# A two-layer encoder with retrieved experts: 32 dense tokens' w_up products turned into row gathers, and sparse gathers brought forward into the retrieval

## The chip, the cores and the metric

The kernel runs on one core of a Trainium2 chip. The metric is the device time of one execution in microseconds (us), the median of the runs shown. A profile is one execution taken by the hardware profiler; its engines are PE (TensorE matmuls; PEld are its weight loads), DVE (VectorE), ACT (ScalarE), POOL (GpSimd) and SP (SyncE, which here only issues DMAs). Each engine works through its own queue in order.

## The reference, cut to what matters

512 tokens of width 1024 pass through two layers. Layer 0 mixes tokens by neighbourhood attention, layer 1 by a short convolution; after either comes the same expert block ("peer"), which takes most of the time:

```
q = (xc @ w_query).reshape(c, PEER_HEADS, 2, PEER_HALF_DIM)
sc = jnp.einsum('chpd,hpnd->chpn', q, keys32)
sv, si = lax.top_k(sc, PEER_TOPK)
...
best, pos = lax.top_k(cand, PEER_TOPK)
eidx = jnp.take_along_axis(cidx, pos, axis=-1)
g = jax.nn.softmax(best, axis=-1)
u = w_up[eidx]
a = jnp.einsum('cd,chkd->chk', xc, u)
act = jax.nn.gelu(a, approximate=False) * g
vv = w_down[eidx]
return jnp.einsum('chk,chkd->cd', act, vv)
```

Every token picks 8 x 16 = 128 of 16384 experts; an expert is one row of w_up and one of w_down (1024 floats each).

## The kernel before, in words

The 512 tokens are four chunks of 128. Chunk 3 is the **sparse** chunk: for each of its 128 picks k, POOL gathers one row per token from w_up (an indirect DMA of 512 KB into `row`), DVE multiplies it with the normed tokens `hn` and sums (`sq`, L482), and later a gather from w_down is added to `accg` (L491). Those are 256 gathers in each layer. Chunks 0 to 2 (TD = 384 tokens) are **dense**: all 16384 experts are computed for all 384 tokens, and a gate matrix that is zero where an expert wasn't picked masks the rest.

The dense part of a layer runs over 128 blocks of 128 experts. An **up** (`dense_up`) loads 512 KB of w_up, splits it into a rounded half on ACT (`wu_h`) and the rest on DVE (`wu_l`, L106), and runs 24 matmuls with 384 columns (`ps_up`, L127), whose Gelu goes to `ab`; the first NPRE = 52 blocks are parked in DRAM (`ad`). A **down** (`dense_down`) multiplies `ab` with the gates `gt`, splits the product and 512 KB of w_down (`wd_l`), and runs 18 matmuls with 512 columns into six PSUM banks that stay open over the layer (`acc`, L541).

A layer of the expert block runs through these stages. In the **query** stage 16 blocks of w_query are multiplied and DVE takes top-16 lists. In the **selection**, DVE works for each chunk through `select`, some 80 small instructions, which give picks and gates. In the **gate products**, for each four dense tokens (a quad, 96 in all) DVE builds one-hot matrices from the picks (`ob`, `oa`), scaled by the gate on ACT or DVE, PE multiplies them (`ps_gb`, four float32 matmuls, two records each in the profile), and ACT copies the result to `stage`, from which `gd` is written to DRAM. In the **experts** stage the downs of all 128 blocks run, the ups that are left and the 256 gathers.

Ups of the first 52 blocks are interleaved with selection and gate products by a planner's ratio: `retrieval` yields estimates of DVE and PE time, and ups are put in until PE's estimate reaches PRE_RATE times that of DVE. In the experts stage ups run AHEAD blocks ahead, and gathers are spread by LATE. Tiles come from pools with a set number of buffers (`wu_h` 2, `wu_raw` and `wd_raw` 3), and a scheduler that estimates times itself places each engine's instructions in their final order, so the order below is that of the built program and not of the source.

## Time and profile before

| what | value |
|---|---|
| median of 3 runs | 2993.33 us (2993.03 to 2993.86) |
| profiled execution, own time | 2994.69 us |
| its span (first to last instruction) | 2992.9 us |
| PE busy | 2952.2 us (99%) |
| DVE busy | 2345.6 us (78%) |
| ACT busy | 1360.9 us (45%) |
| POOL busy | 663.4 us (22%) |

Own time is 1.8 us more than the span and 1.4 us above the median of the runs. Busy time of PE counts a matmul that waits in the pipeline as busy, so how dense PE is must be read from the distance between matmuls, not from its share.

### The profile page before, as it was taken

What the parts mean: (1) busy time and instruction counts of PE and PEld (TensorE: products, weight loads), DVE (VectorE), ACT (ScalarE), POOL (GpSimd) and SP (SyncE); (2) the same over time, 40 slices, a digit from 0 to 9 for tenths busy, and PEclk for the clock granted to TensorE, in tenths of its full rate; (3) what the DMA queues carried; (4) which work ended last, traced back from release to release, by engine and by line L of the source; (5) the groups of instructions that cost most, each with busy time, mean ns of one, the idle gap of its engine ahead of it and who ended that gap; (6) DMA issues with size and microseconds to landing.
All of it is one profiled execution on the core that took longest, in us unless ns stands there. A gap on an engine that the chain in (4) does not pass through costs nothing.

```text
span 2992.9 us, 43780 instructions
## 1 busy us (share of the span) xinstructions
PE 2952.2 (99%) x15570; PEld 2636.1 (88%) x15570; DVE 2345.6 (78%) x5115; ACT 1360.9 (45%) x2237; POOL 663.4 (22%) x571
## 2 busy tenths in 40 slices
PE   8999999999999999999999999999999999999998
PEld 6777899999888888888878789999988888888886
DVE  5445999886888888878864489998788888888786
ACT  5453257994333333333332323699733333333333
POOL 0000000002343444343400000000043434444341
PEclk9999999999999999999999999999999999999999
DMA  5323355659999999999933324556799999999995
GB/s 187 106 81 96 95 161 168 240 214 328 335 337 346 335 343 329 337 343 324 320 113 93 117 87 129 166 216 217 261 352 348 334 347 332 338 330 346 325 329 190
DMA packets 297979, 747.93 MB, mean 250 GB/s; under 512 B 23456, under 2 KB 139168, under 8 KB 294688
## 3 DMA queue, kind: packets, MB, share of 16 engines
q1 hardware_dynamic: 224032, 476.67, 46.5%
q0 software_dynamic: 73728, 268.47, 24.7%
q8 instruction: 122, 2.00, 0.3%
q14 instruction: 97, 0.79, 0.1%
HBM read 672.17 MB, written 72.88 MB: 249 GB/s over the span
## 4 chain that ended last, share of the span: by engine, by line
PE 91%; DVE 4%; issue 2%; DMA 2%; ACT 1%; POOL 0%; DVEq 0%; POOLq 0%; SPq 0%
PE ps_up L127 45%; PE acc L541 33%; PE ps_gb L462 6%; PE ps_o L191 3%; DVE wu_l L106 1%; PE ps_k L403 1%; PE ps_s L260 1%; PE ps_o L300 1%; DMA row<-in_up,eidx 1%; PE ps_pt L286 1%; DMA gd<-stage 0%; PE ps_t L175 0%; POOL row L475 0%; DVE tk L600 0%; ACT sq L150 0%
## 5 line engine op out<-in xcount | busy, mean ns | idle before, releaser
L127 PE MATMUL ps_up<-xhf,wu_l 128*128 128x384 f32 (+1 forms) x2304 | 798.4, 347 | 1.1 <-DVE wu_l L106 1.0
L127 PE MATMUL ps_up<-xhf,wu_h 128*128 128x384 f32 (+1 forms) x2304 | 794.3, 345 | 2.3 <-ACT ab L504 2.0
L127 PE MATMUL ps_up<-xlf,wu_h 128*128 128x384 f32 (+1 forms) x2304 | 792.4, 344 | 0.0
L105 ACT ACTIVATE wu_h<-wu_raw 128x1024 fp32r<-128x1024 f32 x336 | 355.4, 1058 | 688.8 <-PE ps_up L127 413.2
L475 POOL DMA_INDIRECT row<-in_up,eidx x256 | 325.1, 1270 | 1277.9 <-DMA wu_raw<-in_up_t 848.5
L541 PE MATMUL acc<-wd_h,w_l 128*128 128x512 f32 x1536 | 601.4, 392 | 0.1
L541 PE MATMUL acc<-wd_l,w_h 128*128 128x512 f32 x1536 | 601.2, 391 | 0.0
L105 ACT ACTIVATE wd_h<-wd_raw 128x1024 fp32r<-128x1024 f32 x256 | 271.5, 1061 | 699.2 <-issue 591.0
L106 DVE TENSOR_TENSOR wu_l<-wu_raw,wu_h 128x1024 fp32r<-128x1024 f32 x336 | 411.1, 1224 | 191.2 <-ACT wu_h L105 190.1
L541 PE MATMUL acc<-wd_h,w_h 128*128 128x512 f32 x1536 | 513.0, 391 | 0.9 <-ACT w_h L105 0.9
L106 DVE TENSOR_TENSOR wd_l<-wd_raw,wd_h 128x1024 fp32r<-128x1024 f32 x256 | 313.6, 1225 | 231.3 <-ACT wd_h L105 230.7
L127 PEld LDWEIGHTS ps_up<-xhf,wu_h 128*128 128x128 f32 x2304 | 433.3, 188 | 20.9 <-ACT ab L504 3.4
L127 PEld LDWEIGHTS ps_up<-xlf,wu_h 128*128 128x128 f32 x2304 | 433.1, 188 | 17.3
L127 PEld LDWEIGHTS ps_up<-xhf,wu_l 128*128 128x128 f32 x2304 | 433.1, 188 | 16.8 <-DVE wu_l L106 3.8
L475 POOL DMA_INDIRECT row<-in_down,eidx x256 | 332.4, 1298 | 510.4 <-DVE sq L482 471.8
L541 PEld LDWEIGHTS acc<-wd_h,w_l 128*128 128x128 f32 x1536 | 288.2, 188 | 59.5 <-DVE w_l L106 1.2
L491 DVE SCALAR_TENSOR_TENSOR accg<-row,ag,accg 128x1024 f32<-128x1024 f32 x256 | 327.9, 1281 | 15.8 <-DMA row<-in_down,eidx 15.1
L541 PEld LDWEIGHTS acc<-wd_l,w_h 128*128 128x128 f32 x1536 | 288.3, 188 | 59.0
L541 PEld LDWEIGHTS acc<-wd_h,w_h 128*128 128x128 f32 x1536 | 287.0, 188 | 55.3 <-ACT w_h L105 2.3
L482 DVE SCALAR_TENSOR_TENSOR sq<-row,hn 128x1024 bf16<-128x1024 f32 x256 | 312.5, 1221 | 6.2 <-DMA row<-in_up,eidx 5.0
L462 PE MATMUL ps_gb<-ob,oa 128*128 128x128 f32 x1536 | 209.4, 274 | 0.0
L463 ACT ACTIVATE stage<-ps_gb 128x512 f32<-128x512 f32 x192 | 204.5, 1114 | 2.0 <-PE ps_gb L462 1.4
(162 smaller groups left out, 3262.6 us busy)
## 6 DMA issues: line engine op xcount, KB each, us to landing
wd_raw<-in_down SPq DMA_DIRECT2D x256, 512.0 KB, 6.0
wu_raw<-in_up_t SPq DMA_DIRECT2D x256, 512.0 KB, 5.1
gd<-stage SPq DMA_DIRECT2D x24, 2048.0 KB, 7.2
gt<-gd SPq DMA_DIRECT2D x64, 768.0 KB, 9.6
ad<-ab SPq DMA_DIRECT2D x104, 192.0 KB, 2.4
at<-ad SPq DMA_DIRECT2D x52, 384.0 KB, 8.1
wu_raw<-in_w_query SPq DMA_DIRECT2D x32, 512.0 KB, 3.5
wu_raw<-in_w_qkv SPq DMA_DIRECT2D x24, 512.0 KB, 3.7
```

The costliest lines, as they stand in the source:

```text
L105: nc.scalar.activation(hi, raw, AF.Copy)
L106: nc.vector.tensor_tensor(lo, raw, hi.bitcast(F32), op=ALU.subtract)
L127: nc.tensor.matmul(ps[:, :n], a[:, c], b[:, kc, :n], start=k == 0, stop=k == 3 * KC - 1)
L191: nc.tensor.matmul(ps[c], a[:, m, c * P:(c + 1) * P], b, start=m == 0 and i == 0, stop=m == KC - 1 and i == 2)
L260: nc.tensor.matmul(ps[hh][:, a * 256:(a + 1) * 256], t["q"][hs, j * P:(j + 1) * P], kk[hs, :, BAND0[j]:BAND0[j] + BAND], start=True, stop= ...
L286: nc.tensor.transpose(pt[:, i * P:(i + 1) * P], sc[:, a, half * P:(half + 1) * P], ident)
L462: nc.tensor.matmul(ps[:, n * NK:(n + 1) * NK], a, b4[:, n], start=True, stop=True)
L463: nc.scalar.activation(stage[:, :, 4 * q:4 * q + 4].rearrange("p i t -> p t i"), ps.rearrange("p (t i) -> p t i", t=4), AF.Copy)
L475: nc.gpsimd.indirect_dma_start(out=t, out_offset=None, in_=table, in_offset=bass.IndirectOffsetOnAxis(ap=eidx[:, k:k + 1], axis=0))
L482: nc.vector.scalar_tensor_tensor(o, t, 1.0, hn, op0=ALU.mult, op1=ALU.mult, accum_out=ag[:, k:k + 1])
L491: nc.vector.scalar_tensor_tensor(accg, t, ag[:, k:k + 1], accg, op0=ALU.mult, op1=ALU.add)
L541: nc.tensor.matmul(acc[c, half], aa[:, cs], ww[:, hs], start=new and i == 0, stop=n == NK - 1 and ww is held[-1][-1])
```

## The change

Of the 384 dense tokens, the last UT = 32 (the end of chunk 2) no longer take part in the ups: ups have TU = 352 columns. For these 32 tokens the rows of w_up are gathered as for the sparse chunk. The 32 tokens and four groups of 32 picks fill the 128 partitions, so 32 gathers (`urow`) with a multiply and sum each (`sq,au`, L469) do all of their 128 picks; the products, through Gelu and times the gate, become the values with which their one-hots are scaled, and where `ab` has no column for them it holds 1. Their down products stay dense. Chunk 2 is selected first, and the 32 gathers are spread over the selection of the others.

Of the 256 sparse gathers, EARLY = 44 move ahead of the experts stage (`erow`): by the source 20 go between the gate products, and 24 into the seam after them. NPRE grows from 52 to 72, so that 20 more ups belong to the retrieval. One DVE instruction builds all eight one-hots of a quad (`hot`, 1024 elements); ACT scales all four in the first half of the dense tokens, and two in the second half, where DVE scales the other two (L534). `stage` is written in runs of four elements. Blocks are parked and multiplied with gates in pairs; `gt` is loaded for eight blocks at a time instead of four; AHEAD grows to 10; matmuls of the first ups after the gate products are queued behind the last gate product on PE.

```diff
-NPRE = 52
-PRE_RATE = 1.4
+NPRE = 72
+
+
+UN = 1
+UT = 32
+TU = TD - UN * UT
+GB = 8
+PRE_RATE = 1.26
 OB = 12
-ACTN = 2
...
+EARLY = 44
...
-LATE = 0.97
-AHEAD = 4
+LATE = 0.94
+AHEAD = 10
...
-            r3 = rstd_of(c3)
-            nc.vector.scalar_tensor_tensor(hn, h[:, c3], r3, hn, op0=ALU.mult, op1=ALU.mult)
+            nc.vector.scalar_tensor_tensor(hn, h[:, c3], rs[c3], hn, op0=ALU.mult, op1=ALU.mult)
+            cu = ND - 1
+            hu = []
+            for u in range(UN):
+                q = slice(P - (UN - u) * UT, P - (UN - u - 1) * UT)
+                t = wpool.tile([P, D], F32, name="hu", tag="wd_h", bufs=2)
+                nc.sync.dma_start(t[q], g_ffn_row[l].to_broadcast([UT, D]))
+                nc.vector.scalar_tensor_tensor(t[q], h[q, cu], rs[cu][q], t[q], op0=ALU.mult, op1=ALU.mult)
+                for g in range(P // UT):
+                    if g * UT != q.start:
+                        nc.scalar.activation(t[g * UT:(g + 1) * UT], t[q], AF.Copy)
+                hu.append((q, t))
...
+            def unit_lists(gg, ii, jj):
+
+                flat_ids(eid, ii, jj)
+                for u, (q, _) in enumerate(hu):
+                    for g in range(P // UT):
+                        ks = slice(g * UT, (g + 1) * UT)
+                        nc.scalar.activation(fu[ks, u], eid[q, ks], AF.Copy)
+                        nc.scalar.activation(gu[ks, u], gg[q, ks], AF.Copy)
+                nc.vector.tensor_copy(xu, fu)
...
+            def unit_steps():
+
+                at = [(u, k) for u in range(UN) for k in range(UT)]
+                for n in range(len(at) + 2):
+                    if n < len(at):
+                        u, k = at[n]
+                        t = wpool.tile([P, D], F32, name="urow", tag="wd_r", bufs=RAW)
+                        nc.gpsimd.indirect_dma_start(
+                            out=t, out_offset=None, in_=up,
+                            in_offset=bass.IndirectOffsetOnAxis(ap=xu[:, u, k:k + 1], axis=0))
+                        urows.append(t)
+                    if n >= 2:
+                        u, k = at[n - 2]
+                        o = acts.tile([P, D], BF16, name="sq", tag="sq")
+                        nc.vector.scalar_tensor_tensor(o, urows.pop(0), 1.0, hu[u][1], op0=ALU.mult, op1=ALU.mult,
+                                                       accum_out=au[:, u, k:k + 1])
+                    yield
...
+            def unit_values():
+
+                nc.scalar.activation(au, au, AF.Gelu)
+                nc.vector.tensor_tensor(au, au, gu, op=ALU.mult)
+                ps = ps_acc("ps_u")
+                for u in range(UN):
+                    nc.tensor.transpose(ps[:UT, u * P:(u + 1) * P], au[:, u], ident)
+                for u in range(UN):
+                    for g in range(P // UT):
+                        ks = slice(g * UT, (g + 1) * UT)
+                        nc.scalar.activation(gT[ks, TU + u * UT:TU + (u + 1) * UT],
+                                             ps[:UT, u * P + g * UT:u * P + (g + 1) * UT], AF.Copy)
...
-                for c in (3, 0, 1, 2):
+                units = iter(())
+                for c in (cu, c3, 0, 1):
                     it = select(sv[:, c], si[:, c], pr, cand)
                     while True:
                         try:
                             yield next(it), 0.0
+                            for _ in itertools.islice(units, 1):
+                                yield 1.3, 0.0
...
+                            units = itertools.chain(us, itertools.islice(every(3, early), 60))
...
+                    if t0 == TU:
+                        for _ in us:
+                            yield 1.3, 0.0
...
+                        hot = pr.tile([P, 2, 4, NK], F32, name="hot", bufs=OB // 4)
+                        nc.vector.tensor_tensor(hot, iota[:, None, None, :].to_broadcast([P, 2, 4, NK]),
+                                                ijT[:, :, t:t + 4, None].to_broadcast([P, 2, 4, NK]),
+                                                op=ALU.is_equal)
                         for n in range(4):
-                            a, t = a4[:, n], t0 + 4 * q + n
-                            if n < ACTN:
-                                nc.scalar.activation(a, a, AF.Copy, scale=gT[:, t:t + 1])
+                            a = hot[:, 1, n]
+                            if n < 2 or t0 < TD // 2:
+                                nc.scalar.activation(a, a, AF.Copy, scale=gT[:, t + n:t + n + 1])
                             else:
-                                nc.vector.tensor_scalar(a, iota, jT[:, t:t + 1], gT[:, t:t + 1],
-                                                        op0=ALU.is_equal, op1=ALU.mult)
-                            nc.tensor.matmul(ps[:, n * NK:(n + 1) * NK], a, b4[:, n], start=True, stop=True)
-                        nc.scalar.activation(stage[:, :, 4 * q:4 * q + 4].rearrange("p i t -> p t i"),
-                                             ps.rearrange("p (t i) -> p t i", t=4), AF.Copy)
-                        yield 1.35, 0.9
+                                nc.vector.tensor_scalar(a, a, gT[:, t + n:t + n + 1], None, op0=ALU.mult)
+                            last = nc.tensor.matmul(ps[:, n * NK:(n + 1) * NK], a, hot[:, 0, n],
+                                                    start=True, stop=True)
+                        gb.append(last.ins)
+                        nc.scalar.activation(stage[:, :, 4 * q:4 * q + 4],
+                                             ps.rearrange("p (t i) -> p i t", t=4), AF.Copy)
+                        yield 1.0, 0.9
...
+            ring = [pp.tile([P, 2, TD], F32, name=f"ab{n}") for n in range(AHEAD // 2 + 1)]
+            for t in ring:
+                nc.gpsimd.memset(t[:, :, TU:], 1.0)
...
+            def early_steps():
+
+                uses = []
+                for n in range(EARLY + 2):
+                    if n < EARLY:
+                        fn, k = gathers[n]
+                        uses.append(fn(k, wpool.tile([P, D], F32, name="erow", tag="wd_r", bufs=RAW)))
+                    if n >= 2:
+                        uses.pop(0)()
+                    yield
...
-                for ps in up_pieces(up_t[l, b], xh, xl, TD):
+                for ps in up_pieces(up_t[l, b], xh, xl, TU):
                     yield
-                a = pp.tile([P, TD], F32, name="ab", tag="ab", bufs=AHEAD + 2)
-                nc.scalar.activation(a, ps[:, :TD], AF.Gelu)
-                if b < NPRE:
-                    nc.sync.dma_start(ad[b // 2, :, b % 2], a)
-                else:
-                    ab[b] = a
+                a = ring[b // 2 % len(ring)]
+                nc.scalar.activation(a[:, b % 2, :TU], ps[:, :TU], AF.Gelu)
+                if b % 2:
+                    if b < NPRE:
+                        nc.sync.dma_start(ad[b // 2], a[:, :, :TU])
+                    else:
+                        ab[b - 1] = a
...
+                if b % GB == 0 and n:
+                    load_gates(b)
+                if b % 2 == 0:
+                    if b < NPRE:
+                        at = parked[b // 2 % 2]
+                        nc.sync.dma_start(at[:, :, :TU], ad[b // 2])
+                        ab[b] = at
+                    w = p2.tile([P, 2, TD], F32, name="w", bufs=1)
+                    mark = nc.vector.tensor_tensor(w.rearrange("p i (g c) -> p i g c", c=GT),
+                                            ab.pop(b).rearrange("p i (g c) -> p i g c", c=GT),
+                                            first[-1][:, :, b % GB:b % GB + 2].rearrange("p g i c -> p i g c"),
+                                            op=ALU.mult)
+                    pair.append((mark, *split(w, [P, 2, TD], "w", "w", pool=p2)))
+                mark, a_h, a_l = pair[-1]
+                a_h, a_l = a_h[:, b % 2], a_l[:, b % 2]
...
+                    with tc.issue_after(gb[-1]):
+                        for i, _ in enumerate(ups(nup, top)):
+                            if i % 4 == 3:
+                                next(early, None)
+                            if n == 0 and i == 4 * KC - 1:
+                                load_gates(b)
...
-                while ng < len(gathers) and ng * (2 * NK - NPRE) * LATE < done * len(gathers):
+                while ng < len(gathers) and (ng - EARLY) * (2 * NK - NPRE) * LATE < done * (len(gathers) - EARLY):
```

The built order shows where these instructions came to stand.

DVE in the selection of layer 0, before (`cand`, `best`, `msk`, `jj` and the like are tiles of `select`; `wu_l` is the split of an up):

```order
L106 TENSOR_TENSOR wu_l<-wu_raw,wu_h 128x1024
L601 MAX best<-tk 128x8
L608 TENSOR_TENSOR cand<-sv 128x8x16
L608 TENSOR_TENSOR cand<-sv 128x8x8
L608 TENSOR_TENSOR cand<-sv 128x8x5
L608 TENSOR_TENSOR cand<-sv 128x8x4
L602 MAX_INDEX pos<-best,tk 128x8
L608 TENSOR_TENSOR cand<-sv 128x8x3
L608 TENSOR_TENSOR cand<-sv 128x8x2 x3
L610 TENSOR_TENSOR cand<-sv 128x8x8
L627 CAST sf<-si 128x256
L650 TENSOR_TENSOR msk<-msk 128x128x2
```

The same stretch of DVE's queue with the change:

```order
L113 TENSOR_TENSOR wu_l<-wu_raw,wu_h 128x1024
L469 SCALAR_TENSOR_TENSOR sq,au<-urow,hu 128x1024
L726 MAX_INDEX pos<-best,tk 128x8 x2
L744 TENSOR_TENSOR g<-best 128x128
L776 TENSOR_TENSOR jj<-msk 128x128
L113 TENSOR_TENSOR wu_l<-wu_raw,wu_h 128x1024
L469 SCALAR_TENSOR_TENSOR sq,au<-urow,hu 128x1024
L756 CAST pf<-pos 128x128
L722 MAX best<-cand 128x8 x3
L441 SCALAR_TENSOR_TENSOR eid<-ii,jj 128x128
L722 MAX best<-cand 128x8 x2
```

Multiply-and-sum instructions of the 32 tokens (`urow`) now stand between the rows of the selection, about one for each split of an up.

PE at the end of the gate products of layer 0, before (one row of four gate matmuls, then matmuls of ups):

```order
L462 MATMUL ps_gb<-ob,oa 128x128
L127 MATMUL ps_up<-xlf_2382,wu_h 128x384
L462 MATMUL ps_gb<-ob,oa 128x128 x3
L127 MATMUL ps_up<-xhf_2381,wu_l 128x384
L127 MATMUL ps_up<-xhf_2381,wu_h 128x384
L127 MATMUL ps_up<-xlf_2382,wu_h 128x384
L462 MATMUL ps_gb<-ob,oa 128x128 x4
```

The same place with the change:

```order
L535 MATMUL ps_gb<-hot 128x128 x6
L134 MATMUL ps_up<-xlf_2382,wu_h 128x352
L134 MATMUL ps_up<-xhf_2381,wu_l 128x352
L535 MATMUL ps_gb<-hot 128x128 x93
L479 MATMUL ps_u<-ident,au 32x128
L535 MATMUL ps_gb<-hot 128x128 x35
L134 MATMUL ps_up<-xhf_2381,wu_h 128x352
L134 MATMUL ps_up<-xlf_2382,wu_h 128x352
```

The gate products of the last 32 quads (128 matmuls) now stand in one piece, with no matmul of an up between them; all 72 ups of the retrieval are ahead of them.

DVE in the last third of the gate products, before (`ob` and `oa` are the one-hots of a quad):

```order
L460 TENSOR_SCALAR oa<-iota,jT,gT 128x128 x2
L106 TENSOR_TENSOR wu_l<-wu_raw,wu_h 128x1024
L448 TENSOR_TENSOR ob<-iota,iT 128x512
L452 TENSOR_TENSOR oa<-iota,jT 128x256
L460 TENSOR_SCALAR oa<-iota,jT,gT 128x128 x2
```

The same with the change (`erow` is a sparse gather brought forward, `wd_l` the split of a down's weights):

```order
L526 TENSOR_TENSOR hot<-iota,ijT 128x1024
L574 SCALAR_TENSOR_TENSOR accg<-erow,ag,accg 128x1024
L113 TENSOR_TENSOR wd_l<-wd_raw,wd_h 128x1024
L526 TENSOR_TENSOR hot<-iota,ijT 128x1024 x2
L534 TENSOR_SCALAR hot<-hot,gT 128x128 x2
L113 TENSOR_TENSOR wd_l<-wd_raw,wd_h 128x1024
L534 TENSOR_SCALAR hot<-hot,gT 128x128 x4
L526 TENSOR_TENSOR hot<-iota,ijT 128x1024 x2
L534 TENSOR_SCALAR hot<-hot,gT 128x128 x2
```

A quad is now one `hot` of 1024 elements and two scalings of 128; the uses of all 44 gathers that were brought forward stand ahead of the last `hot`, in the gate products, and not in the seam.

## Rows read from the trace of the kernel before

**Rows 1.** The page: busy by engine, clock and DMA in 40 slices.

```profile
PE 2952.2 (99%) x15570; PEld 2636.1 (88%) x15570; DVE 2345.6 (78%) x5115; ACT 1360.9 (45%) x2237; POOL 663.4 (22%) x571
...
PEclk9999999999999999999999999999999999999999
DMA  5323355659999999999933324556799999999995
```

**Rows 2.** Busy time by stage, layer 0: selection, gate products, seam, experts.

```profile
368.80:475.80 107.00, 105.46 (x602) 102.72 (x601) 106.52 (x497) 57.47 (x70) 0.00 (x0) 1.00 0.50 159
475.80:690.00 214.20, 214.20 (x1509) 214.09 (x1508) 189.53 (x444) 196.14 (x348) 0.00 (x0) 1.00 0.60 213
690.00:706.80 16.80, 16.59 (x97) 16.27 (x96) 3.69 (x5) 5.97 (x9) 4.29 (x4) 1.00 0.88 294
706.80:1420.00 713.20, 713.20 (x3473) 632.15 (x3474) 584.83 (x766) 254.95 (x374) 294.62 (x228) 1.00 0.96 340
1420.00:1528.00 108.00, 107.90 (x512) 93.25 (x511) 86.30 (x116) 41.48 (x60) 32.40 (x24) 1.00 0.79 279
```

**Rows 3.** The chain that ended last, in order of time: an up, two downs.

```profile
764.71 4.18 PE ps_up L127 x24
...
810.43 8.20 PE acc L541 x36
```

**Rows 4.** Timeline of PE in the gate products: eight records are a quad.

```profile
602.61 1.05 PE L462 MATMUL ps_gb<-ob,oa 128*128 128x128 f32 x8
603.42 0.42 PE L127 MATMUL ps_up<-xhf,wu_l 128*128 128x384 f32 x1
603.68 0.34 PE L127 MATMUL ps_up<-xhf,wu_h 128*128 128x384 f32 x1
```

**Rows 5.** Timeline of DVE: selection, then gate products (start, length).

```profile
399.61 0.22 DVE L660 TENSOR_SCALAR field<-pf 128x128 f32<-128x128 bf16 x1
399.74 0.23 DVE L663 TENSOR_SCALAR step<-pf 128x128 f32<-128x128 bf16 x1
...
403.16 1.23 DVE L106 TENSOR_TENSOR wu_l<-wu_raw,wu_h 128x1024 fp32r<-128x1024 f32 x1
404.29 1.23 DVE L643 TENSOR_TENSOR msk<-msk,ds 128x2048 bf16<-128x2048 bf16 x1
...
603.46 0.68 DVE L448 TENSOR_TENSOR ob<-iota,iT 128x512 f32<-128x512 f32 x1
604.06 0.42 DVE L452 TENSOR_TENSOR oa<-iota,jT 128x256 f32<-128x256 f32 x1
604.39 0.60 DVE L460 TENSOR_SCALAR oa<-iota,jT,gT 128x128 f32<-128x128 f32 x2
604.91 0.69 DVE L448 TENSOR_TENSOR ob<-iota,iT 128x512 f32<-128x512 f32 x1
```

**Rows 6.** Groups by line and form, DVE and ACT.

```profile
L482 DVE SCALAR_TENSOR_TENSOR sq<-row,hn 128x1024 bf16<-128x1024 f32 x256 | 312.5, 1221 | 6.2 <-DMA row<-in_up,eidx 5.0
L277 DVE TENSOR_SCALAR sc<-sc,sm 128x256 f32<-128x256 f32 x64 | 19.6, 351 | 0.8
L169 DVE TENSOR_SCALAR hs<-h,r 128x1024 f32<-128x1024 f32 x16 | 11.8, 748 | 0.1
L463 ACT ACTIVATE stage<-ps_gb 128x512 f32<-128x512 f32 x192 | 204.5, 1114 | 2.0 <-PE ps_gb L462 1.4
L458 ACT ACTIVATE oa<-oa,gT 128x128 f32<-128x128 f32 x384 | 130.5, 390 | 28.0 <-DVE oa L452 27.9
L400 ACT ACTIVATE qpT<-ps_up 128x512 f32<-128x512 f32 x32 | 18.6, 580 | 0.0
```

**Rows 7.** Gathers: length of POOL's instruction (min/median/max), landing, and three in time.

```profile
L475 POOL DMA_INDIRECT row<-in_up,eidx x256: 932/1011/3282, 699.6 to 2914.8; - x128
...
row<-in_up,eidx POOLq DMA_INDIRECT x256, 7.6
...
1001.71 0.94 POOL L475 DMA_INDIRECT row<-in_down,eidx  x1 [1.66 <-DVE sq L482]
1005.84 1.86 POOL L475 DMA_INDIRECT row<-in_up,eidx  x1 [3.19 <-DVE accg L491]
```

**Rows 8.** Busy time and granted clock around an idle PE, and in a half-full stretch.

```profile
266.50:270.00 3.50, 3.42 (x18) 3.45 (x19) 3.08 (x16) 0.91 (x4) 0.00 (x0) 0.55 0.10 40
...
458.00:464.00 6.00, 5.00 (x28) 4.47 (x28) 6.00 (x15) 3.30 (x8) 0.00 (x0) 1.00 0.44 146
```

More of the change, by code (lines that the diff above doesn't have):

```diff
@@ new lines, in retrieval @@
+                            last = nc.tensor.matmul(ps[:, n * NK:(n + 1) * NK], a, hot[:, 0, n],
[4 more added lines that the diff above has]
+                        yield 1.0, 0.9
+                        for _ in itertools.islice(units, 1):
+                            yield 1.3, 0.0
@@ L548, in ups, with every @@
                     yield from dense_up(b)
+            def every(n, it):
+                for k in itertools.count():
+                    if k % n == 0:
+                        next(it, None)
+                    yield
+            early = early_steps()
+            gb = []
             dve = pe = 0.0
@@ L560, in peer @@
             p2 = st.enter_context(tc.tile_pool(name="experts", bufs=2))
-            fresh = list(range(NPRE // 4, NK // 4))
-            kept = list(range(NPRE // 4))
+            fresh = list(range(NPRE // GB, NK // GB))
+            kept = list(range(NPRE // GB))
             order = []
@@ L566, in peer @@
                 order.append(q)
-                while len(kept) and (NPRE // 4 - len(kept)) * len(fresh) <= n * (NPRE // 4):
+                while len(kept) and (NPRE // GB - len(kept)) * len(fresh) <= n * (NPRE // GB):
                     order.append(kept.pop(0))
             order += kept
-            blocks = [4 * q + i for q in order for i in range(4)]
-            ng = done = 0
+            blocks = [GB * q + i for q in order for i in range(GB)]
+            parked = [p2.tile([P, 2, TD], F32, name=f"at{n}", bufs=1) for n in range(2)]
+            for t in parked:
+                nc.gpsimd.memset(t[:, :, TU:], 1.0)
+            ng = EARLY
+            done = 0
             rows = [p2.tile([P, D], F32, name=f"row{n}", bufs=1) for n in range(RING)]
```

92 lines of the change are left out of this document (46 added, 46 removed).

## The prediction

> **What bounds the kernel now.** I read the page first: PE is busy for 99% of the span, at the full clock in every slice [rows 1]. Since a waiting matmul counts as busy, I went on to the table by stage and to distances between matmuls. The reader should see there that two stages have two full engines. In the selection of layer 0 DVE is busy for 106.5 of 107.0 us [rows 2]; in the gate products PE is full and DVE has 25 us to spare; in the experts stage PE is full, DVE is not, and the DMA engines are 96% busy. That PE is truly dense shows in the chain: an up takes 4.18 us for 24 matmuls (0.174 us each), two downs 8.20 us for 36 (0.228 us) [rows 3]; so 70 to 75 ups and 2304 down matmuls fill the experts stage from the last gate product at 690.0 to 1528.0 us: 75 x 4.18 + 2304 x 0.228 = 838.4 against 838.0. No wait of PE is there to be removed; the change can gain only by less PE work, and loses wherever PE now waits.
>
> **What it saves.** From 512 to 384 columns a matmul falls from 0.228 to 0.174 us, 0.00042 us a column [rows 3]. At 352 that gives 0.161 us, so 3.86 us for an up instead of 4.18: 0.32 x 128 = 41 us of PE in a layer, 82 us in all. Bounds: proportional to columns it would be 0.1595 us (4 us more a layer). The other end is no gain at all, if the weight load set the pace; the gate products speak against that, where records with a weight load each follow at some 0.11 us (a quad's eight take 603.68 - 602.61 - 0.174 = 0.896 us [rows 4]).
>
> **What it adds, and where.** I count instructions between marks in the built order of layer 0 (layer 1 differs by one or two), and take durations from rows. Back to back, DVE's instructions follow closer than they last: a split 1.13 us (404.29 - 403.16), a quad's one-hots 1.45 us (604.91 - 603.46) [rows 5].
>
> *Part A, from the first split of a retrieval up to the 42nd: DVE sets the time.* Before, the selection stretch holds 24 splits (27.1), three quads (4.4), hence 75 us of selecting; in the gate stretch, 189.5 us busy less 93 quads (134.9) and 31 splits (35.0) leave at most 19.6 us more of it [rows 2, 5]. In the new order all but some 5 us of that stand ahead of the 42nd split, so 85 to 90; I take 86. With it stand 42 splits (47.5), 31 of the 32 new multiply-and-sums at about 1.2 us, a bit under their 1.22 us [rows 6] (37.2), and 11 `hot` instructions. One `hot` has the 1024 elements of a split, so 1.13 us; at most twice the 512-element 0.60 us (604.06 - 603.46), 1.20. Sum: 86 + 47.5 + 37.2 + 12.4 = 183 us. PE has 42 x 3.86 + 9.5 quads x 0.9 = 171 us of work there and waits for 12.
>
> *Part B, up to the 70th up: PE sets the time.* 28 ups and 50 quads: 108.1 + 45 = 153 us. DVE has 28 splits, 50 `hot`, 35 uses of gathers brought forward, one of the new ones, 24 scalings and 5 us of selection: 31.6 + 56.5 + 43.2 + 4.8 + 5 = 141 us, hidden. ACT has 50 copies into `stage`, most quads with four scalings, and 28 ups. The copy with runs of four elements is in no row: between 0.58 us (contiguous) and 1.11 us (single elements) [rows 6]; even the upper end leaves ACT at about PE's time, so it costs nothing in either case.
>
> *Part C, to the last gate product: DVE sets the time again, and PE is bare.* Of its work only two ups and 36 quads are left, 41 us; what covered this stretch before, an up for every four quads, is used up. DVE has 35 `hot` (39.6), nine gather uses (10.8), six splits (6.8) and 72 scalings of 128 elements. Their price: 256 elements last 351 ns and 1024 last 748 [rows 6], so 128 would last 285, back to back some 0.20; bounds 0.13 (399.74 - 399.61, a plain 128-element step) and 0.26 (two of the old two-step ones, in 604.91 - 604.39) [rows 5]. With 0.20: 14.4. Sum 72 us, of which PE idles about 31. One more us passes to the last gate product.
>
> *Part D, the experts stage.* 56 ups and all downs: 216 + 525 = 741 us. The seam's wait for `gd` and `gt` lies behind five ups, as it lay behind four. The moved gathers take DMA out of this stage, but the last 34 downs have no up beside them; by the order, 24 gathers fall to 16 of these downs, 25 MB in 66 us, over the 340 GB/s at 96% of the DMA engines [rows 2]. Three buffers for each kind of load take most of that up; bounds 0 and 5 us, I take 1.
>
> *Start of the block.* The 32 tokens' normed rows cost DVE one instruction of the size of a multiply (1.2 us) in the query stage and ACT three copies; one norm computed twice before is dropped. I take 1 us of loss, between 0 and 2.
>
> **The sum.** After: 183 + 153 + 72 + 1 + 741 + 1 + 1 = 1152 us a layer. Before, between the same marks, 1528.0 - 368.8 = 1159 us [rows 2]. That is 7.4 us less a layer before rounding, 15 in two layers: 41 us of matmuls are saved, and about 33 come back as waits of PE in A and C. The profiled execution's own 2994.7 us becomes 2980; it lies 1.4 us above the median, so 2978 us for the median.
>
> **Rivals.** *Late gathers (slower).* A use on DVE frees a buffer, POOL issues (0.93 to 3.28 us), and the rows land a median of 7.6 us later in the full experts stage [rows 7]: with the use 9.7 us at least, for three uses. In A they come every 3.4 us or so, 10.3 us for three. For the landing speaks that DMA was half idle here (0.50 share [rows 2]); against it, that with gathers this share rises to about nine tenths, and that in an in-order queue everything behind a late use waits, splits above all. In B 12 us of slack hide it, in A and C nothing does: 40 uses at 0.5 us are 20 us a layer, so 2978 + 40 = 3018. It decides from 0.19 us a use on. The POOL instruction took 0.94 us and, with DVE at work, 1.86 us in neighbouring rows [rows 7].
>
> The Trainium skill, page "SBUF — State Buffer", section "SBUF: two separate sides", says that a DMA issued from GpSimd can't write its descriptors while DVE runs an operation in a two-port mode, which a float32 scaling or copy may be, though not an operation with two tensor inputs. By that rule only the new scalings in C would delay gathers, by less than one instruction each, and the sum stays; the longer POOL rows here stand beside instructions with two tensor inputs, so the trace shows more delay than the page would give.
>
> *DVE dearer (no change).* `hot` at 1.20 and scalings at 0.26 us add 0.8 + 2.5 + 4.3 us a layer and leave 2993.
>
> *PE's clock.* In C PE works 41 of 72 us in pieces. The clock was granted at 0.55 after a wait without any work (between 1.2 and 2.4 GHz), and stayed at 1.00 in a stretch with 5.00 of 6 us busy by the page but only 28 matmul records [rows 8]; nothing shows a half-idle PE for 50 us. At 1.2 GHz a quad takes 1.8 us, below DVE's 2.0, so only the first ups behind it pay, some 3 us a layer: 2984.
>
> The Trainium skill, page "TensorE: Matmul & The Clock Gate", section "What's actually happening", says that the gate throttles a PE that isn't kept busy; the trace agrees for the wait in [rows 8].
>
> *All cheap (faster).* Scalings at 0.13, matmuls proportional, selection at 85: 10 us less a layer, 2958.
>
> *It doesn't do what it says.* If 352 columns cost as much as 384, the later ups alone add 40 us a layer: over 3050.
>
> **Chances.** The sum as it stands, 2968 to 2986 with the clock's variant: 0.42; all cheap 0.16; no change by dearer DVE work or gathers a little late 0.20; late gathers or DMA in the tail, over 2999, 0.19; no cheaper matmul 0.03. What this measurement can tell from no change is about 0.2%, 6 us. Faster 0.58, same 0.20, slower 0.22. The range from 2952 to 3010 leaves out the dearest half of late gathers and little below.
>
> **What would show it.** Right: matmuls of an up 0.161 us apart; DVE full from the first selection to the 42nd up; 128 gate matmuls in a row at half density for 55 to 65 us, with PE waiting for DVE's scalings; an experts stage of about 741 us without waits. Wrong: DVE waiting for `urow` or `erow` for more than 8 us a layer, ACT ending PE's waits in the gate products, or holes in PE over the last 34 downs.

## The result, and the profile after

The changed kernel takes 3035.8 us (median of four runs, 3029.4 to 3043.8) against 2993.3 us: a ratio of 1.0143, 95% interval 1.013 to 1.0155. It is slower by 42 us where 15 less were forecast, and outside the range. The four runs differ by 14 us, those of before by 0.8. The profiled execution is the slowest of them, 3043.8 us with a span of 3042.0.

The page of the changed kernel, to be held against [rows 1]:

```profile
PE 2915.6 (96%) x15572; PEld 2584.5 (85%) x15572; DVE 2370.8 (78%) x4602; ACT 1330.4 (44%) x2327; POOL 827.2 (27%) x651
...
PE   8998999998899999999899999899989999999998
...
DMA  5321259898699999999823224789869999999995
```

PE is no longer at 9 in every slice. Where the holes are shows in the table by stage (start:end, length, then busy time of PE, PEld, DVE, ACT, POOL; granted clock, DMA share, GB/s), as in [rows 2]. The first two rows are part A of layer 0, then B, C, the seam, and the experts stage in two pieces, cut at its last up; the last two are A and B of layer 1:

```profile
373.50:478.40 104.90, 99.92 (x611) 97.03 (x610) 100.91 (x439) 54.26 (x71) 14.86 (x13) 1.00 0.64 212
478.40:561.20 82.80, 77.91 (x500) 76.02 (x499) 79.59 (x168) 49.18 (x91) 25.28 (x21) 1.00 0.84 289
561.20:712.30 151.10, 151.10 (x1063) 151.08 (x1062) 142.10 (x177) 117.77 (x287) 58.72 (x37) 1.00 0.94 344
712.30:786.30 74.00, 59.69 (x371) 53.13 (x369) 71.66 (x128) 51.92 (x125) 7.66 (x7) 0.91 0.70 265
786.30:813.00 26.70, 19.75 (x125) 19.46 (x123) 5.58 (x5) 7.10 (x11) 4.64 (x6) 0.91 0.90 321
813.00:1380.40 567.40, 566.59 (x2820) 499.94 (x2821) 455.79 (x517) 202.98 (x258) 239.79 (x171) 1.00 0.93 334
1380.40:1550.60 170.20, 160.69 (x709) 132.99 (x707) 127.89 (x145) 57.09 (x68) 54.18 (x38) 0.97 0.80 286
1849.50:2041.20 191.70, 179.33 (x1103) 174.82 (x1102) 181.56 (x612) 103.75 (x160) 49.70 (x34) 0.98 0.72 244
2041.20:2203.60 162.40, 157.15 (x1081) 156.37 (x1080) 143.23 (x178) 117.86 (x291) 64.26 (x38) 0.98 0.89 323
```

The prediction's sum by these marks, in us (experts stage: from the last gate product to the last down; start: how much later than before the first split comes, in layer 1 counted from the end of layer 0):

| term | predicted | layer 0 | layer 1 |
|---|---|---|---|
| start | +1 | +4.7 | +5.5 |
| A | 183 | 187.7 | 191.7 |
| B | 153 | 151.1 | 162.4 |
| C, with its one more | 73 | 74.0 | 71.3 |
| experts, with its one more | 742 | 764.3 | 755.0 |
| sum | 1152 | 1181.8 | 1185.9 |

The two layers miss by 64 us together: 35 in the experts stage, 21 in A and B, 8 at the start. That is all of the difference between 2980 and 3043.8.

What PE and DVE waited for there (engine, line, tile, what ended the wait: us in all, times, longest). PE in the experts stage of layer 0 up to its last up, and behind it; DVE in A of layer 0, in A of layer 1, and in B of layer 1:

```profile
PE acc L645 <- ACT w_h L112: 7.0, 1, 7.0
...
PE acc L645 <- ACT wd_h L112: 9.5, 2, 8.1
...
DVE sq L469 <- DMA urow<-in_up,xu: 6.1, 3, 3.5
...
DVE sq L469 <- DMA urow<-in_up,xu: 9.3, 3, 4.7
...
DVE sq L564 <- DMA erow<-in_up,eidx: 8.8, 3, 4.3
```

All five go back to a transfer that came late. The chain that ended last names it for both waits of PE in the experts stage (start, length, what), and three stretches of the table show what the second one cost:

```profile
793.59 9.59 DMA gt<-gd
...
1459.81 17.30 DMA wd_raw<-in_down
```

```profile
1466.00:1478.00 12.00, 4.24 (x19) 3.19 (x17) 4.61 (x5) 1.66 (x2) 2.59 (x2) 0.82 1.03 400
1478.00:1490.00 12.00, 11.71 (x40) 9.43 (x41) 9.63 (x12) 3.10 (x4) 4.72 (x3) 0.75 0.71 247
1490.00:1502.00 12.00, 12.00 (x55) 9.94 (x54) 10.68 (x12) 5.84 (x8) 4.96 (x4) 1.00 0.85 275
```

PE stands still while the DMA engines run without a gap, at 400 GB/s, and afterwards its clock is granted at 0.75, so it ran in part at the lower of its two levels (1.2 and 2.4 GHz): 40 records in 12 us, where 55 stand in the next, undisturbed stretch. The idle time is thus paid a second time, in part.

### The profile page after: what moved, and what is told of

Read it like the earlier page. It is cut to its first block, busy times and chain, and to the rows that moved or that the text cites. A ratio compares the mean times of both kernels' runs of the same rounds, so it can differ in the third digit from the quotient of the medians.

```text
span 3042.0 us, 43151 instructions
## 1 busy us (share of the span) xinstructions
PE 2915.6 (96%) x15572; PEld 2584.5 (85%) x15572; DVE 2370.8 (78%) x4602; ACT 1330.4 (44%) x2327; POOL 827.2 (27%) x651
## 4 chain that ended last, share of the span: by engine, by line
PE 70%; issue 14%; DMA 8%; DVE 5%; ACT 1%; POOL 1%; DVEq 0%; POOLq 0%; ACTq 0%; SPq 0%
PE ps_up L134 31%; PE acc L645 30%; PE ps_gb L535 4%; PE ps_o L199 3%; DMA wd_raw<-in_down 2%; DMA urow<-in_up,xu 1%; DMA row<-in_down,eidx 1%; DVE hot L526 1%; DMA row<-in_up,eidx 1%; DMA gd<-stage 1%; DMA erow<-in_up,eidx 1%; DVE wu_l L113 1%; PE ps_s L268 1%; PE ps_o L308 1%; DMA gt<-gd 1%
## 5 line engine op out<-in xcount | busy, mean ns | idle before, releaser
L134 PE MATMUL ps_up<-xhf,wu_l 128*128 128x352 f32 (+1 forms) x2304 | 772.6, 336 | 16.9 <-DVE wu_l L113 16.5
L134 PE MATMUL ps_up<-xhf,wu_h 128*128 128x352 f32 (+1 forms) x2304 | 774.0, 336 | 9.0 <-ACT ab L599 4.7
L134 PE MATMUL ps_up<-xlf,wu_h 128*128 128x352 f32 (+1 forms) x2304 | 766.7, 333 | 0.0
L645 PE MATMUL acc<-wd_h,w_h 128*128 128x512 f32 x1536 | 602.9, 394 | 27.6 <-ACT wd_h L112 16.2
L645 PE MATMUL acc<-wd_l,w_h 128*128 128x512 f32 x1536 | 506.7, 390 | 0.0
L555 POOL DMA_INDIRECT row<-in_down,eidx x216 | 299.5, 1387 | 396.9 <-DVE sq L564 344.0
L574 DVE SCALAR_TENSOR_TENSOR accg<-row,ag,accg 128x1024 f32<-128x1024 f32 x216 | 276.7, 1281 | 24.6 <-DMA row<-in_down,eidx 23.6
L564 DVE SCALAR_TENSOR_TENSOR sq<-row,hn 128x1024 bf16<-128x1024 f32 x208 | 253.7, 1220 | 13.0 <-DMA row<-in_up,eidx 11.4
L535 PE MATMUL ps_gb<-hot 128*128 128x128 f32 x1536 | 228.0, 291 | 33.8 <-DVE hot L534 18.1
L535 PEld LDWEIGHTS ps_gb<-hot 128*128 128x128 f32 x1536 | 208.8, 200 | 47.8 <-DVE hot L534 27.4
```

Source lines behind the costliest of these rows:

```text
L134: nc.tensor.matmul(ps[:, :n], a[:, c], b[:, kc, :n], start=k == 0, stop=k == 3 * KC - 1)
L535: last = nc.tensor.matmul(ps[:, n * NK:(n + 1) * NK], a, hot[:, 0, n], start=True, stop=True)
L555: nc.gpsimd.indirect_dma_start(out=t, out_offset=None, in_=table, in_offset=bass.IndirectOffsetOnAxis(ap=eidx[:, k:k + 1], axis=0))
L564: nc.vector.scalar_tensor_tensor(o, t, 1.0, hn, op0=ALU.mult, op1=ALU.mult, accum_out=ag[:, k:k + 1])
L574: return lambda: nc.vector.scalar_tensor_tensor(accg, t, ag[:, k:k + 1], accg, op0=ALU.mult, op1=ALU.add)
L645: nc.tensor.matmul(acc[c, half], aa[:, cs], ww[:, hs], start=new and i == 0, stop=n == NK - 1 and ww is held[-1][-1])
```

## The experiments

All times are medians; the profiled execution of each gives its stages.

**Single edits.** Four edits of the changed kernel, each against one suspect. The first loads each `gt` in two halves:

```diff
-                gt = p2.tile([P, TD // GT, GB, GT], F32, name="gt")
+                if b % GB == 0:
+                    first.append(p2.tile([P, TD // GT, GB, GT], F32, name="gt"))
...
-                if b % GB == 0 and n:
+                if b % 4 == 0 and n:
```

> The changed kernel, but each `gt` of eight blocks is loaded as two transfers of 0.77 MB, the second four blocks later. Theory 'bursts of gt': in the seam PE waits 7.3 and 4.7 us for the first product with gt, whose one transfer of 1.5 MB lands 9.6 us after the last gd; with half of it the waits fall under 2 us, and the w_down loads queued behind a gt in the last 40 downs (17.3 us and 15.3 us to land, against about 8) come sooner, so most of the 10.3 and 6.7 us of holes there go too. Median 3036 down by 20 to 30, to about 3010. Rival 'too many gathers in the tail': only the seam gets better, the holes in the tail stay: down by 8 to 14, to about 3025. Rival 'gt is not it': within 5 us of 3036.

Measured: 3035.6 us (3026.8 to 3039.6). The wait in the seam, counted here from the start of one matmul to the start of the next (0.3 us more than the idle time), fell from 7.3 to 1.6 us; in layer 1 the 4.7 us for `gt` went, and an up waited 1.8 us for its split instead. But the last downs still had holes of 10.7 and 7.5 us, and the time did not move beyond its scatter. Halving `gt` mends the seam and not the tail.

The second was to move `hu`: its block of code went into the query loop (`if hp == 8:`).

> The changed kernel, but the rows `hu` of the 32 tokens (one DVE instruction, three ACT copies) are made in the middle of the query stage instead of ahead of its first matmuls. Theory: the three ACT copies (3.2 us) stand ahead of the first copies of `xhf`, PE waits 2.4 us for them and then runs its next 6 us at half clock, so the first up of the retrieval comes 4.7 us later than before in layer 0 and 5.5 us in layer 1 (relative to the end of layer 0). Here both go: 3036 down by 9 to 11, to about 3026. Rival: the delay is from the DVE chain of the norms, and stays: within 3 us of 3036.

Measured: 3039.6 us (3037.4 to 3043.4). The scheduler put the instructions back: in the built order nothing had moved, so this is the changed kernel once more, and tells only its scatter. With the order written out (`with tc.issue_after(...)` on DVE and on ACT):

> The changed kernel with the rows `hu` of the 32 tokens made behind the third block of the query stage by an explicit order on DVE and on ACT (in the run before this one the scheduler had put them back to the old place, in the built order nothing had moved). Theory: the DVE instruction (1.28 us, ahead of the last `hs`) and the three ACT copies (3.19 us, ahead of the first `xhf`) make the first query matmul 2.4 us late and keep the next 6 us at half clock; here the first up of layer 0 comes at about 369 instead of 373.2 to 373.5 us, and the same in layer 1: 3036 to 3040 down by 9 to 11, to about 3028. Rival: the start stays at 373 and the time within 4 us.

Measured: 3022.7 us (3020.4 to 3029.6). The first split of layer 0 comes at 370.0 instead of 373.5 us, that of layer 1 294.3 us behind the end of layer 0 instead of 298.9. That is 8 us of the gain; the other 5 are within the scatter. ACT's timeline of the changed kernel shows the cause, the first query matmul of PE's timeline the result, in the changed kernel and then in this one (start, length; in brackets the idle time before and what ended it):

```profile
269.57 3.19 ACT L408 ACTIVATE hu<-hu 32x1024 f32<-32x1024 f32 x3 [3.33 <-DVE hu L405]
272.78 4.15 ACT L186 ACTIVATE xhf<-ps_t,gf 128x512 fp32r<-128x512 f32 x7
```

```profile
273.52 1.22 PE L134 MATMUL ps_up<-xhf,wu_h 128*128 128x512 f32 x2 [2.13 <-ACT xhf L186]
```

```profile
272.25 0.73 PE L134 MATMUL ps_up<-xhf,wu_h 128*128 128x512 f32 x2 [0.23 <-ACT xhf L186]
```

The third edit left the 32 tokens' gathers out (`urows.append(hn)` in place of the indirect DMA):

> The changed kernel without the 32 gathers of w_up for the 32 tokens in each layer: their multiply-and-sums read a resident tile instead (so the values of these 32 tokens are left out of the computation; all DVE work stays). Theory 'late gathers': DVE waits 6.1 us (layer 0) and 9.3 us (layer 1) for urow and PE waits about as long for the splits behind it, so the stretch to the 42nd split falls from 188 and 192 us to about 182 in both layers, and with 33 MB less to move the 44 early gathers come in time too: 3036 down by 15 to 30, to about 3014. Rival 'DVE alone sets the pace': the stretch stays at 188 or more; within 6 us of 3036.

Measured: 3024.4 us (3021.1 to 3028.5); part A 181.7 and 188.5 us. The waits for `urow` are gone, but the scheduler also placed ups differently (A of layer 1 stayed long), so this supports late gathers without isolating them. The fourth spread the gathers of the experts stage by the ups that really run:

```diff
-                done += 1 if b < NPRE else 2
-                while ng < len(gathers) and (ng - EARLY) * (2 * NK - NPRE) * LATE < done * (len(gathers) - EARLY):
+                done += 1 + (0 if n == 0 or b < NPRE else 2 * (nup - seen))
+                seen = nup
+                while ng < len(gathers) and (ng - EARLY) * (NK + 2 * (NK - NPRE - AHEAD - 1)) * LATE < done * (len(gathers) - EARLY):
```

> The changed kernel with the sparse gathers of the experts stage spread by the ups that really run then (three gathers for a down with an up beside it, one for a down without), instead of two shares for every fresh block, whose ups have run ten blocks ahead. The 45 gathers of the last 34 downs become 21. Theory 'too many gathers in the tail': 19 gathers fall to eight downs without ups (15.7 MB in 33 us, 476 GB/s wanted against 340); spread out, the holes of 10.3 and 6.7 us in the last 170 us and the half clock behind them (some 3 us) go: 3036 down by 15 to 22, to about 3018. Theory 'bursts of gt': the holes stay, as each gt of 1.5 MB still stands ahead of a w_down load: within 6 us of 3036.

Measured: 3028.3 us (3022.1 to 3043.4), holes of 5.1 and 4.5 us over the last downs instead of 10.3 and 6.7. Half the expected gain, and not beyond the scatter. The built order says why the run decides little: the gathers behind the last up, which were to become fewer than half, stayed as many (41 issues on POOL in layer 0, against 38 in the changed kernel).

**Parts undone.** What the experts stage loses to transfers as a whole:

> The changed kernel without the transfers of the 212 gathers of each layer's experts stage (left out of the computation; the instructions that use them stay and read a tile filled once). All else has its place in the order. Theory 'transfers': with 111 of 247 MB gone nothing comes late there, the stretch from the last gate product to the last down falls from 764 and 755 us to 741 of matmuls plus a wait in the seam that stays, some 5 to 8 us: about 748 in both layers, the holes over the last 40 downs are gone; 3036 to 3040 down by 20 to 25, to about 3015. Rival 'order and clock': the holes come from the order of DVE and ACT work, the stretch stays at 755 to 764; within 6 us.

Measured: 3009.1 us (3006.9 to 3010.4). The experts stage takes 741.8 and 741.4 us, the predicted matmuls to the microsecond, and the seam's wait goes too. Its table, behind the seam of layer 0 and for the whole stage of layer 1:

```profile
806.00:1528.10 722.10, 721.33 (x3528) 628.89 (x3526) 579.08 (x657) 259.83 (x326) 0.00 (x0) 1.00 0.57 180
2255.10:2996.50 741.40, 741.02 (x3651) 648.46 (x3649) 582.52 (x660) 264.57 (x333) 3.81 (x6) 1.00 0.57 180
```

DVE and ACT have the same instructions, so their work is not the cause; POOL's issuing of the gathers went together with the transfers. `gt` is still loaded in one piece of 1.5 MB here, so what made PE wait in the seam was that burst together with the gathers beside it. Next, the gathered tokens undone (`UN = 0`, the selection starting with chunk 3 again):

> One part undone alone: no 32 gathered tokens, ups have 384 columns again (24 early gathers, the pairs, `gt` of eight blocks, 72 ups ahead, the one-hots in one instruction all stay). Worked out by the terms of the prediction: ups 0.32 us dearer, DVE 38 us less in the selection, which PE then bounds: about 347 us to the 70th up instead of 339 to 354, 73 to the last gate product, 759 of matmuls plus some 10 us of waits in the experts stage with the same bytes as now: about 1188 us a layer against 1177 to 1180, less 5 us at the start: 3036 to 3040 up by about 10, 3035 to 3060. Theory: the narrower ups pay a little, the loss comes from the rest (transfers pressed together). Rival 'the 32 tokens' gathers are the loss': without them the kernel is at 3020 or below.

Measured: 3040.6 us (3034.7 to 3044.2). From the first split to the last down 1179.8 and 1182.3 us, against 1177.1 and 1180.4. But the edit did not undo this part alone. With the 32 tokens' gathers gone, the early ones, 44 and not 24, moved up into the selection: in the first 212.7 us of layer 0 DVE has 39 uses of `erow`, where part A of the changed kernel has 31 of `urow`, and waits 14.2 us for them:

```profile
L567 DVE SCALAR_TENSOR_TENSOR sq<-erow,hn 128x1024 bf16<-128x1024 f32 x23 | 28.0, 1217 | 7.6 <-DMA erow<-in_up,eidx 7.6
L577 DVE SCALAR_TENSOR_TENSOR accg<-erow,ag,accg 128x1024 f32<-128x1024 f32 x16 | 20.4, 1276 | 6.6 <-DMA erow<-in_down,eidx 6.6
```

So DVE was not relieved as expected, and what the narrower ups with their gathers are worth by themselves is not shown by any run. What the run does show is a kernel without them that loses as much, 47 us against the kernel before. Then only the early gathers undone (`EARLY = 0`):

> One part undone alone: no gathers brought forward, all 256 run in the experts stage. Theory 'the transfers bound the experts stage': DVE is 53 us a layer lighter in the retrieval, of which B (full of PE work) gives nothing back but its late gathers and C 11 us, so the retrieval gets 12 to 20 us shorter, while the experts stage has 23 MB more to move, 270 MB at 340 GB/s: 793 us instead of 755 to 764. Sum: 3036 to 3040 up by 25 to 50, about 3075. Rival 'the holes in the experts stage come from order, not from its bytes': the stage stays under 775, and the kernel gets faster, 3010 to 3030.

Measured: 3123.0 us (3120.4 to 3133.9), more than expected, and in another place. The downs end after 759.8 us, as with the early gathers, but then the sparse tokens' gathers go on alone for 60 us (layer 1: 55):

```profile
773.50:1533.30 759.80, 744.60 (x3651) 650.91 (x3649) 601.78 (x683) 265.68 (x335) 326.20 (x231) 0.99 0.94 335
1533.30:1593.40 60.10, 0.00 (x0) 0.00 (x0) 42.11 (x52) 2.10 (x5) 33.62 (x27) 0.54 0.79 261
```

So with 256 gathers in the stage the matmuls lose no more than with 212; the queue of gathers falls behind. With 20 more ups in the retrieval the stage is too short for all of them, and some have to come forward.

**Three buffers or ten blocks ahead.** With `AHEAD = 4` memory is free for five buffers of raw rows (`tag="wd_r", bufs=5`), with uses of `urow` and `erow` four behind their issue instead of two:

> The changed kernel with five buffers instead of three for the gathered rows and the raw w_down blocks, the uses of the gathers four behind their issue instead of two; ups run 4 blocks ahead in the experts stage instead of 10, which gives the memory for it. Theory 'a gather takes longer than three uses last': with five, DVE waits for urow and erow under 2 us a layer instead of 6.7 and 19.8, the stretch to the 42nd split falls from 188 and 192 us to 182 to 184, the one behind it in layer 1 from 162 to about 154; and the last downs without ups become some 20 instead of 34: 3036 to 3040 down by 20 to 30, to about 3013. Rival 'the transfers themselves are too slow there': DVE waits stay, the stretches stay at 187 to 192 and 162; only the tail changes, by 10 at most.

Measured: 2994.7 us (2989.8 to 3009.0), 41 less, for the same bytes. The experts stage of layer 0:

```profile
778.50:1520.20 741.70, 741.11 (x3653) 648.74 (x3652) 589.43 (x664) 268.50 (x337) 296.50 (x214) 1.00 0.92 332
```

Layer 1 takes 749.6 us, 6.3 of them the wait for `gt`. DVE's waits fell from 15.4 to 10.8 us for `urow` and from 11.7 to 4.3 for `erow`; what is left for `urow` are three waits of up to 4.7 us, the longest at the first use behind the first issue, which no buffer shortens. With `AHEAD = 4` alone:

> The changed kernel with one number other: ups run 4 blocks ahead in the experts stage instead of 10 (three buffers and uses two behind, as in the change). It takes apart the run with five buffers, which gave 2994.7 us. Theory 'ups too far ahead': the last downs without an up fall from 34 to 20, so the crowd of gathers meets fewer of them; the experts stage falls from 764 and 755 to 742 to 750, the retrieval stays at 413 and 425: about 3010. Theory 'three buffers are too few': the holes stay, as w_down blocks can be called only three ahead: 3030 to 3038.

Measured: 3023.1 us (3022.1 to 3028.6): the experts stage takes 748.5 and 750.8 us, with 4.4 and 4.6 us of wait in the seam and single holes of up to 2.7 us in the tail; A and B stay at 187.5, 189.4, 151.1 and 163.0. So running ups ten blocks ahead made most of the holes in the tail, and the longer rings give the rest: 14 and 8 us in the profiled executions of these two kernels, most of them behind A (B and C together 225.1 to 221.3 and 234.4 to 225.5 us) and in layer 0's experts stage. The 28 us between the medians are more than these 22; the rest lies within the scatter.

**Versions meant to beat both.** `combo` joins `gt` in halves, `hu` late, the spread gathers and 80 ups in the retrieval; the `d` and `f` versions have five buffers and ups 4 ahead instead, with 64 or 72 ups and 20 to 44 gathers brought forward.

> A version meant to beat both: the changed kernel with `gt` in halves, sparse gathers spread by the ups that really run, `hu` out of the way, and 80 ups in the retrieval at a planner's rate of 1.05, so that they reach into the last third of the gate products (32 of 96 quads without ups become 8 to 12). By the counts of the built order: 417 us of retrieval, 710 us of matmuls in the experts stage, which then has 243 MB to move (715 us at 340 GB/s): 1132 us a layer, with 20 us of late transfers 1150, against 1159 before. Theory: 2993 down by 10 to 30, about 2975. Rival 'the transfers are the bound in both stages': what is taken from one stage comes back in the other, 3000 to 3020.

Measured: 2999.2 us (2990.3 to 3005.3, ratio 1.0012, 1.0 to 1.0025): ups reach C, but B grows from 151.1 to 162.8 us in layer 0, and the tail has holes again, 11.6 us.

> A version that asks less of DVE in the retrieval and less of the transfers behind it: the changed kernel with 64 ups and 20 gathers ahead of the experts stage instead of 72 and 44, `gt` in halves, gathers spread by the ups that run, `hu` out of the way, five buffers, ups 4 blocks ahead. Counts of its built order: 367 us of retrieval (DVE), 772 us of matmuls in the experts stage with 261 MB (768 us at 340 GB/s). With some 15 us of waits 1154 us a layer, against 1159 before: 2993 down by 0 to 20, about 2983. Rival 'any such version runs into the transfers': 2995 to 3015.

Measured: 2983.7 us (2981.8 to 2988.1; 0.9966, 0.9954 to 0.9979).

> The same with 72 ups and 20 gathers ahead: 385 us of retrieval, 741 us of matmuls in the experts stage, but 259 MB to move (761 us at 340 GB/s), so there the transfers should set the time: 385 + 761 + 10 = 1156 us a layer, and the experts stage 755 to 770 although its matmuls are 741. 2993 down by 0 to 15, about 2987. If the transfers do not bound it, the stage takes 745 and the kernel 2960.

Measured: 3003.7 us (2998.9 to 3011.5). The downs take the 742 us of their matmuls at 339 GB/s, and the sparse tokens' last use ends 33 us later, in layer 0 (the second stretch is cut 2 us behind it):

```profile
763.60:1505.70 742.10, 741.03 (x3651) 648.71 (x3649) 594.78 (x671) 264.56 (x333) 315.15 (x226) 1.00 0.96 339
1505.70:1541.00 35.30, 0.01 (x1) 0.00 (x0) 24.46 (x30) 3.33 (x6) 17.05 (x17) 0.57 0.67 221
```

> All four mends on the changed kernel (five buffers with ups 4 ahead, `gt` in halves, gathers by the ups that run, `hu` out of the way), with its 72 ups and 44 early gathers, planner's rate 1.0. By counts: 399 us of retrieval and 741 us of matmuls, 247 MB in the experts stage (742 us at the 333 GB/s that it reached in four kernels): 1140 plus some 15 us of late gathers and seam, 1155 a layer. Theory: 2975 to 2988. Rival 'the mends overlap': no better than the 2994.7 of the five buffers.

Measured: 2968.5 us (2965.9 to 2972.0; 0.9917, 0.9904 to 0.9931), 26 us below the five buffers alone. The planner's rate (1.0 instead of 1.26) changed with the mends; no run tells its share. A, B, C and the experts stage of layer 0, and the experts stage of layer 1:

```profile
369.70:554.00 184.30, 177.25 (x1112) 172.92 (x1110) 181.20 (x609) 104.53 (x164) 47.56 (x36) 1.00 0.77 262
554.00:723.10 169.10, 164.22 (x1129) 161.95 (x1129) 161.05 (x206) 126.20 (x307) 67.72 (x41) 0.99 0.94 347
723.10:775.50 52.40, 44.45 (x303) 39.80 (x301) 50.97 (x97) 41.05 (x102) 0.00 (x0) 0.97 0.58 227
775.50:1516.40 740.90, 740.90 (x3653) 648.95 (x3652) 589.40 (x664) 267.91 (x336) 297.51 (x214) 1.00 0.94 333
2213.00:2954.60 741.60, 741.23 (x3651) 648.66 (x3649) 585.48 (x660) 264.06 (x333) 302.08 (x214) 1.00 0.93 328
```

> The same with 32 early gathers and a faster pace of the others (0.88), since with 20 of them and 0.94 the sparse chain ended 33 us (layer 0) and 23 us (layer 1) behind the last down. By counts 386 us of retrieval; 253 MB at 333 GB/s are 760 us, more than the 741 of matmuls: 1146 plus 10 to 15, 1158 a layer. Theory 'the rate of the transfers bounds the experts stage': 2985 to 3000, no better than 44 early gathers, and the chain of sparse gathers ends at or behind the last down. If it is below 2978, that rate is not the bound.

Measured: 2967.2 us (2964.5 to 2969.5; 0.9909, 0.9894 to 0.9924), no worse, so the 333 GB/s in that expectation was what those kernels asked for and not the limit. Here the stage ran at 338 GB/s and its sparse tokens ended 8.3 us behind the last down in layer 0, 2.8 ahead of it in layer 1: the edge is about there.

## Why the prediction was wrong

**Right.** The cheaper matmul: 46 follow each other in 7.41 us, 0.161 each, and two downs still take 8.16 us (rows of the chain):

```profile
828.90 7.41 PE ps_up L134 x46
...
894.45 8.16 PE acc L645 x36
```

The prices on DVE: a `hot` 1.13 to 1.14 us, a new scaling 0.196, a multiply-and-sum of `urow` 1.14 apart (predicted 1.13, 0.20, 1.2). DVE's work in A is 180.5 us (100.91 + 79.59) and 181.6 in layer 1, against 183. B in layer 0 and C in both layers came within 2 us, C with PE waiting for DVE's and ACT's scalings. The copy into `stage` is 592 ns, at its lower bound.

**Wrong, the experts stage.** The step was: "by the order, 24 gathers fall to 16 of these downs, 25 MB in 66 us" and "bounds 0 and 5 us, I take 1". The stage cost 22 and 13 us more: 7.3 and 4.7 in the seam, 10.3 and 6.7 as holes over the last downs, and much of the rest in matmuls at the lower clock behind them. `no_rows` shows that transfers are all of it. `ahead4` shows that running ups ten blocks ahead makes most of the holes (10.3 us became 1.0 in layer 0, 6.7 became 3.7 in layer 1), and `deep5` that with more loads called ahead the same bytes leave no hole over the last downs. Why the tail and not earlier stretches is argued from a count and not shown: by the source 19 gathers fall to eight downs whose ups are already done (15.7 MB in 33 us, 476 GB/s), which a mean over 16 downs hid; in the trace no 33 us of layer 0's tail hold more than 12 issues.

**Wrong, the seam.** "The seam's wait for `gd` and `gt` lies behind five ups, as it lay behind four": `gt` of eight blocks is 1.5 MB instead of 0.77, and PE waited 7.3 and 4.7 us. `gt_halves` took most of that away, and so did leaving out the gathers beside it (`no_rows`, where DVE's first product with `gt` starts at 803.8 us, against 811.1 in the changed kernel; `gt` is called at 793.7 and 793.6). I had listed the larger `gt` in the change and not costed it.

**Wrong, late gathers.** They stood as a rival at 0.5 us a use, 20 us a layer; the sum had none. DVE waited 6.7 us in A and B of layer 0 and 19.8 in layer 1. That B's 12 us of slack hide them was wrong in layer 1, where DVE waited three times for an `erow` and the longest wait, 4.3 us, held up `hot`, ACT's scaling and PE in turn (PE for 4.2 us). That is 13 us a layer, or 0.33 us for each of the 40 uses where the rival had 0.5 and was to decide from 0.19 on: A and B together took 21 us more than predicted, enough to turn the forecast gain by itself; how much of that the late gathers are is not isolated (without the 32 tokens' transfers A was 6.0 and 3.2 us shorter). What the prediction says of POOL's issues beside DVE no run isolates either.

**Wrong, the start.** "1 us of loss, between 0 and 2": the copies were priced as busy time, but they stand in ACT's queue ahead of the copies that the first query matmul waits for, and PE then runs largely at half clock (granted 0.58 from 274 to 280 us). 4.7 and 5.5 us; `hu_after` gave 8 of the 10 back.

All three of its signs of being wrong appeared: DVE waited more than 8 us in layer 1 (19.8), ACT ended 15.3 us of PE's waits in the gate products, and PE had holes over the last downs.

So the saving of 41 us a layer was there, by the distance between matmuls, and the sum's 409 us for A, B and C became 413 and 425. With the experts stage and the start, some 32 us a layer more than forecast went to transfers that came late and to the start; for A and B that is the likely cause, not an isolated one. With the order mended (`f_72_44`) a layer takes 1146.7 and 1145.1 us, a little under the predicted 1152, and the kernel 2968.5 us against the 2978 forecast. That fits the sum without these losses; it is another order, though, so the nearness of the two figures proves no single term.

## What to carry to other kernels

Where a stage runs at over 90% of its DMA share, cost a change's bytes in the window of each burst, a few blocks long, and not over the stage; and count how many loads can be called ahead, since rings of three that were enough for even work are not for bursts. An instruction added off the critical path is free only if nothing on the path stands behind it in its engine's queue. Where a scheduler sets the order, look where a moved instruction came to stand before reading anything into a run.

## What the runs showed of the hardware

PE's clock fell without a full stop of PE. From 728 us on, in C of the changed kernel, PE's queue holds gate products alone but for one transposition, and no wait of PE there is longer than 1.7 us. Yet from 732 to 756 us the clock was granted at 0.72 and 0.75, so partly at the lower of its two levels, and at 0.96 and 1.00 in the next stretches. DVE is full in all four rows; in the first two it also had gathers to use and fed PE fewer gate products (42 and 39 records, then 63 and 65):

```profile
732.00:744.00 12.00, 9.35 (x42) 7.78 (x41) 12.00 (x24) 6.77 (x17) 2.79 (x3) 0.72 0.82 312
744.00:756.00 12.00, 8.40 (x39) 7.40 (x40) 12.00 (x20) 7.33 (x17) 0.00 (x0) 0.75 0.80 273
756.00:768.00 12.00, 9.36 (x63) 7.83 (x61) 12.00 (x25) 9.41 (x24) 0.00 (x0) 0.96 0.67 281
768.00:780.00 12.00, 9.62 (x65) 8.08 (x65) 12.00 (x24) 10.29 (x28) 0.00 (x0) 1.00 0.37 157
```

It cost nothing that shows, since DVE set the pace there (12.00 of 12 us; C took 74.0 us against a forecast of 73). The Trainium skill, page "TensorE: Matmul & The Clock Gate", section "What's actually happening", says that activity releases the clock and lack of it throttles; the trace agrees in direction, with the low clock in the stretches in which PE was fed least.

The DMA engines moved 400 GB/s over 12 us and never more than 339 over an experts stage. The Trainium skill, page "DMA: Bandwidth & Descriptors", section "Specifications", gives some 358 GB/s as a core's share of its memory and 435 as the limit of the path to SBUF; the 339 lie under the one, the 400 between the two.
